# Attention heads taken in pairs with products by turns, and GpSimd's work given to VectorE

## The chip, the cores and the metric

One core of a Trainium2 chip runs the whole program. The metric is the device time of one execution in microseconds (us), the median over runs. PE is TensorE's matmul, PEld its weight load, DVE VectorE, ACT ScalarE, POOL GpSimd, SP SyncE, which issues the DMAs.

## The reference, cut to what matters

Two blocks follow each other on one sequence of 256 tokens of width 1024, all in float32.

The first block has two layers over the 256 latent tokens and, in layer 0, 256 context tokens too. Each layer is a modulated norm, an attention, a gated residual, a modulated norm, a SwiGLU feed-forward and a gated residual. Layer 0's attention has 8 latent heads (query and key of 96 rows, 64 + 32, value of 64) and 8 neighbourhood heads (64 rows, with an added bias and a mask on the latent keys); latent queries see 512 keys, context queries the 256 context keys. Layer 1's has 16 window heads of 64 rows that share 2 key heads, with a mask, a sink that enters maximum and sum, and 512 keys.

```python
p = jax.nn.softmax(sc.astype(jnp.float32) * scale, axis=-1)
return jnp.einsum('bqhk,bkc->bqhc', p, c_kv)
```

The second block has two layers of a mixer and an expert feed-forward. The mixer has five branches: pooling, a gated convolution of 31 taps, difference attention (4 heads with two score maps of 32 rows each, out = (softmax1 - lam * softmax2) V), a short convolution and memory attention (4 heads of 64 rows against 256 memory tokens); the branches are normed and projected together. The expert feed-forward scores 128 x 128 keys, picks 16 and sums the experts' outputs.

## The kernel before, in words

Activations lie with features on the 128 partitions and tokens along the free dimension. A weight arrives as a tile of 128 x 1024 (`raw`, three buffers), ACT casts it to a rounded `hi` (L85), and DVE or POOL subtracts to get `lo` (L91); which of the two is set by a pattern such as `lo_pat = "gv"`, g for POOL and v for DVE by turns. Each product is then three matmuls: hi x hi, hi x lo, lo x hi (`mm3`, L149 to L151). Activations are split in the same way (`split`, ACT at L330 and the subtraction at L334).

The program is written once in Python; a list scheduler in the compiler places each engine's instructions by priority, about program order, and by its own estimate of times. Each engine runs its list in order, and semaphores guard the buffers of each named tile. A DMA of SP's queue that waits for a buffer holds back those behind it. `issue_after(x)` puts an instruction behind x on x's engine.

An attention step (`attend`) takes one head: two query tiles of 128 tokens, with their scores S in PSUM banks of tag A (four in all). DVE takes the row maximum (L474), scales it (L476 to L479), ACT exponentiates with a running sum (L482), DVE inverts the sum (L487) and multiplies (L489), PE transposes the 128 x 128 pieces through banks of tag C (two, L495), ACT copies them to `pts` (L498), and PE multiplies them with the values into one half (64 partitions) of a bank of tag B (L500). A plain float32 product shows as two PE records. In layer 0 (`att0`) a loop runs over 8 blocks of two heads, and within it over latent and context queries; neighbourhood heads add their bias by a product with 8 times the identity (L822), after POOL has added the mask to it (L806). In layer 1 (`att1`) a loop runs over 8 blocks of two heads that lie on rows 0 to 63 and 64 to 127. Memory heads (`memattn`, scores at L1259) use `attend` too; the difference heads have their own loop (`diff`, scores at L1221), one call for each head, placed among the mixer's steps by the list `SEQ` (d0 to d3; m0 and m1 are memory heads).

The modulation's columns are made beside all this: `mod_cols` loads 128 x 1024 (`mraw` with two buffers in the first attention, later `raw`) and DVE multiplies it twice with a row, summing the product (L457). 24 of them are spread over the first attention and the projections before it.

## Time and profile before

| what | us |
|---|---|
| median of three runs | 3173.33 |
| lowest and highest | 3170.05, 3173.34 |
| the profiled execution | 3177.91 |
| its span | 3176.1 |
| PE busy | 3037.9 (96%) |
| DVE busy | 2169.0 (68%) |
| ACT busy | 1296.0 (41%) |
| POOL busy | 403.4 (13%) |

The span runs from the first instruction to the last. Busy time is the time in which an engine has at least one instruction under way; matmuls overlap, so a full PE may still be a slow one. The granted clock is the share of full speed that TensorE was given: 1.00 is 2.4 GHz, 0.50 is 1.2 GHz, and a figure between is a mean over both. POOL's work is almost all in the first block, which ends at about 1120 us.

### The profile page before, as it was taken

The page shows a single profiled execution, that of the slowest core. Times are in us where ns is not written, and L with a number is a line of the kernel's source. Part 1 is how long each engine was busy: PE and PEld are TensorE (multiplying, and loading weights), DVE is VectorE, ACT ScalarE, POOL GpSimd, SP SyncE. Part 2 cuts the span into 40 slices and gives each one's busy share as a digit, 9 for nine tenths or more (in the row PEclk, how much of TensorE's full clock was granted, in tenths as well). Part 3 has the DMA queues.
Part 4 walks back from the last instruction along what each step waited for, and adds up shares of the span by engine and source line. Part 5 has one row for each costly group of instructions (what it writes and reads, how often), then busy time and mean ns, then how long its engine had stood idle before and what let it go on. Part 6 is the DMA issues. An engine that isn't in the chain of part 4 may idle for free.

```text
span 3176.1 us, 50064 instructions
## 1 busy us (share of the span) xinstructions
PE 3037.9 (96%) x19574; PEld 2604.6 (82%) x19574; DVE 2169.0 (68%) x4434; ACT 1296.0 (41%) x2194; POOL 403.4 (13%) x214
## 2 busy tenths in 40 slices
PE   8999999998999999899999998999989999999899
PEld 4766877787589987799999986878789999998787
DVE  5777795437564467699884478556669988447854
ACT  4464322224444422344444444443334444443343
POOL 2432344443014400000000000000000000000000
PEclk9999999999799999999999999999989999999999
DMA  7303265543025552355455544554135545554454
GB/s 251 131 21 124 89 199 195 175 146 116 10 78 195 175 176 86 102 178 180 161 170 188 186 153 163 189 179 165 60 111 176 184 162 169 188 188 146 147 189 148
DMA packets 136222, 480.43 MB, mean 151 GB/s; under 512 B 15345, under 2 KB 18161, under 8 KB 135601
## 3 DMA queue, kind: packets, MB, share of 16 engines
q1 hardware_dynamic: 135888, 476.97, 44.2%
q8 instruction: 154, 2.52, 0.3%
q14 instruction: 84, 0.68, 0.1%
q0 software_dynamic: 96, 0.26, 0.0%
HBM read 476.11 MB, written 1.05 MB: 150 GB/s over the span
## 4 chain that ended last, share of the span: by engine, by line
PE 73%; DVE 15%; DMA 5%; issue 4%; ACT 1%; POOL 1%; SPq 0%; DVEq 0%; ACTq 0%; POOLq 0%
PE A L149 7%; PE A L1413 7%; PE A L1412 7%; PE A L1414 7%; PE A L150 6%; PE A L151 6%; PE B L150 6%; PE B L149 6%; PE B L151 6%; PE A L112 4%; DMA raw<-modt 3%; PE B L500 3%; DVE lo L91 2%; PE A L1098 2%; DVE junk L457 2%
## 5 line engine op out<-in xcount | busy, mean ns | idle before, releaser
L85 ACT CAST hi<-raw 128x1024 fp32r<-128x1024 f32 (+1 forms) x733 | 765.2, 1045 | 1358.1 <-PE B L150 327.6
L91 DVE TENSOR_TENSOR lo<-raw,hi 128x1024 fp32r<-128x1024 f32 (+1 forms) x601 | 738.2, 1228 | 451.4 <-ACT hi L85 446.5
L149 PE MATMUL B<-xh,hi 128*128 128x256 f32 x2048 | 575.4, 281 | 0.0
L150 PE MATMUL B<-xl,hi 128*128 128x256 f32 x2048 | 573.1, 280 | 0.0
L151 PE MATMUL B<-xh,lo 128*128 128x256 f32 x2048 | 572.4, 279 | 0.0
L149 PE MATMUL A<-xh,hi 128*128 128x256 f32 (+1 forms) x1200 | 398.0, 334 | 23.3 <-DVE nt L516 11.0
L1413 PE MATMUL A<-hi,al 128*128 128x512 f32 x1024 | 409.5, 400 | 0.2 <-DVE al L334 0.2
L1414 PE MATMUL A<-lo,ah 128*128 128x512 f32 x1024 | 407.5, 398 | 0.0
L1412 PE MATMUL A<-hi,ah 128*128 128x512 f32 x1024 | 396.7, 399 | 4.6 <-ACT ah L330 4.6
L150 PE MATMUL A<-xl,hi 128*128 128x256 f32 (+1 forms) x1200 | 397.7, 332 | 3.5 <-DVE xl L350 2.7
L151 PE MATMUL A<-xh,lo 128*128 128x256 f32 (+1 forms) x1200 | 396.6, 331 | 2.2 <-POOL lo L91 2.2
L91 POOL TENSOR_TENSOR lo<-raw,hi 128x1024 fp32r<-128x1024 f32 (+1 forms) x132 | 324.2, 2458 | 520.5 <-ACT hi L85 520.4
L150 PEld LDWEIGHTS B<-xl,hi 128*128 128x128 f32 x2048 | 385.1, 188 | 3.8
L149 PEld LDWEIGHTS B<-xh,hi 128*128 128x128 f32 x2048 | 385.0, 188 | 3.4
L151 PEld LDWEIGHTS B<-xh,lo 128*128 128x128 f32 x2048 | 384.3, 188 | 0.0
L149 PEld LDWEIGHTS A<-xh,hi 128*128 128x128 f32 x1200 | 232.1, 194 | 48.7 <-issue 18.7
L150 PEld LDWEIGHTS A<-xl,hi 128*128 128x128 f32 x1200 | 232.6, 194 | 24.9 <-DVE xl L350 3.7
L151 PEld LDWEIGHTS A<-xh,lo 128*128 128x128 f32 x1200 | 232.7, 194 | 24.1 <-POOL lo L91 4.7
L1412 PEld LDWEIGHTS A<-hi,ah 128*128 128x128 f32 x1024 | 193.6, 189 | 47.3 <-ACT ah L330 5.3
L1414 PEld LDWEIGHTS A<-lo,ah 128*128 128x128 f32 x1024 | 194.4, 190 | 45.5
L1413 PEld LDWEIGHTS A<-hi,al 128*128 128x128 f32 x1024 | 194.3, 190 | 42.6 <-DVE al L334 1.0
L457 DVE SCALAR_TENSOR_TENSOR junk<-raw,cb 128x1024 bf16<-128x1024 f32 x80 | 124.4, 1555 | 104.4 <-DMA raw<-modt 103.4
(372 smaller groups left out, 4559.8 us busy)
## 6 DMA issues: line engine op xcount, KB each, us to landing
raw<-peer_u SPq DMA_DIRECT2D x256, 512.0 KB, 3.5
raw<-peer_v SPq DMA_DIRECT2D x256, 512.0 KB, 3.5
raw<-w_gu SPq DMA_DIRECT2D x88, 512.0 KB, 3.8
raw<-modt SPq DMA_DIRECT2D x56, 512.0 KB, 3.6
w<-w_in SPq DMA_DIRECT2D x36, 512.0 KB, 4.3
raw<-w_down SPq DMA_DIRECT2D x32, 512.0 KB, 3.6
raw<-peer_wq SPq DMA_DIRECT2D x32, 512.0 KB, 3.5
mraw<-modt SPq DMA_DIRECT2D x24, 512.0 KB, 3.7
```

What stands on the lines that cost most here:

```text
L85: nc.scalar.copy(hi[:, :w], raw[:, :w])
L91: self.last_lo = e.tensor_tensor(out=lo[:, :w], in0=raw[:, :w], in1=hi[:, :w].bitcast(FT), op=OP.subtract)
L112: mm(ps[:, :256], w[:, k * 128:k * 128 + 128], x[:, k], start=k == 0, stop=k == 7)
L149: mm(out, wh, xh, start=start, stop=False)
L150: mm(out, wh, xl, start=False, stop=False)
L151: return mm(out, wl, xh, start=False, stop=stop)
L457: nc.vector.scalar_tensor_tensor(j, raw, 1.0, self.cb[:, v], op0=OP.mult, op1=OP.mult, accum_out=self.M[:, l, b, v:v + 1])
L500: nc.tensor.matmul(o, V(k), pts[:, k], start=k == 0, stop=k == nk - 1)
L1098: nc.tensor.matmul(ps, w[:, s], ch[:, b], start=b == 0, stop=b == 1)
L1412: mm(acc[t][d], ah[:, s], hi[:, ws], start=n == 0, stop=False)
L1413: mm(acc[t][d], al[:, s], hi[:, ws], start=False, stop=False)
L1414: mm(acc[t][d], ah[:, s], lo[:, ws], start=False, stop=n == 127)
```

## The change

Heads are taken two at a time. `attend2` does for two heads what `attend` did for one, and keeps its maxima and sums for both in one small tile; the matmuls of the two heads' scores (`scores2`) and of their products with the values are put in a fixed order in which the heads take turns (`turns`). The latent heads' queries and keys are padded from 96 to 128 rows with zeros. The difference heads become two calls of two heads each, with one maximum, one scaling and one inversion for both, and `SEQ` has d0 and d1 alone. All patterns that sent a subtraction to POOL send it to DVE, as do the mask's sum, the rotation of layer 1's queries and keys, and one norm. `mraw` has one buffer where it had two; `e` has three in the first attention and four elsewhere where it had two.

```diff
-SEQ = (("cg hq mq mh hn dv d0 up d1 mn d2 po cv0 sa d3 r0 mv dh sb m0 r3 w0 dn w3 m1 g0 r2 r4 cv1 w2 cm g3 w4 g2 cn g4 w1 r1 g1").split(),
-       ("hq cg mq hn dv mh d0 up d1 sa po mv mn d2 d3 w0 dh sb m0 r3 r0 w3 dn m1 g3 cv0 r2 cv1 cm g0 w2 g2 w4 cn r4 g4 w1 r1 g1").split())
+SEQ = (("cg hq mq mh hn dv d0 up mn d1 po cv0 sa r0 mv dh sb m0 r3 w0 dn w3 m1 g0 r2 r4 cv1 w2 cm g3 w4 g2 cn g4 w1 r1 g1").split(),
+       ("hq cg mq hn dv mh d0 up sa po mv mn d1 w0 dh sb m0 r3 r0 w3 dn m1 g3 cv0 r2 cv1 cm g0 w2 g2 w4 cn r4 g4 w1 r1 g1").split())
...
-LP1 = "gv"
+LP1 = "v"
...
-QLE = "ggv"
-ALE = "gg"
-NVP = "g"
+QLE = "v"
+ALE = "vv"
+NVP = "v"
...
-        self.lo_pat = "gv"
+        self.lo_pat = "v"
...
-                self.split(xh[:, k, :T], xl[:, k, :T], t, le="g" if k % 2 else "v")
+                self.split(xh[:, k, :T], xl[:, k, :T], t, le="v")
...
-            raw = self.mp.tile([128, WCH], FT, name="mraw", bufs=2)
+            raw = self.mp.tile([128, WCH], FT, name="mraw", bufs=1)
...
+    def attend2(self, S, nk, scale, V, po, sinks=None, bufs=(4, 2)):
+
+
+        nc, ap, v = self.nc, self.atp, self.nc.vector
+        w = nk * 128
+        e = [ap.tile([128, 2, 512], FT, name="e", bufs=bufs[0]) for _ in range(2)]
+        for q in range(2):
+            st = self.sp.tile([128, 5, 2], FT, name="st2", bufs=4)
+            for g in range(2):
+                v.reduce_max(st[:, 0, g:g + 1], S[g][q], axis=AX.X)
+            if sinks is not None:
+                v.scalar_tensor_tensor(st[:, 0], st[:, 0], scale, sinks, op0=OP.mult, op1=OP.max)
+                v.tensor_scalar(st[:, 1], st[:, 0], -1.0, None, op0=OP.mult)
+            else:
+                v.tensor_scalar(st[:, 1], st[:, 0], -scale, None, op0=OP.mult)
+            for g in range(2):
+                nc.scalar.activation(e[g][:, q, :w], S[g][q], AF.Exp, bias=st[:, 1, g:g + 1], scale=scale,
+                                     accum_out=st[:, 2, g:g + 1])
+            if sinks is not None:
+                v.tensor_tensor(out=st[:, 4], in0=sinks, in1=st[:, 0], op=OP.subtract)
+                nc.scalar.activation(st[:, 4], st[:, 4], AF.Exp)
+                v.tensor_tensor(out=st[:, 2], in0=st[:, 2], in1=st[:, 4], op=OP.add)
+            v.reciprocal(st[:, 3], st[:, 2])
+            for g in range(2):
+                v.tensor_scalar(e[g][:, q, :w], e[g][:, q, :w], st[:, 3, g:g + 1], None, op0=OP.mult)
+        pts = [ap.tile([128, 4, 256], FT, name="pts", bufs=bufs[1]) for _ in range(2)]
+        for g in range(2):
+            for kp in range(nk // 2):
+                pt = self.bank("C")
+                for kk in range(2):
+                    for q in range(2):
+                        k = 2 * kp + kk
+                        nc.tensor.transpose(pt[:, kk * 256 + q * 128:kk * 256 + q * 128 + 128],
+                                            e[g][:, q, k * 128:k * 128 + 128], self.ident)
+                nc.scalar.copy(pts[g][:, 2 * kp:2 * kp + 2].rearrange("p a b -> p (a b)"), pt)
+        self.turns([(po[g * 64:g * 64 + 64, :256], V(g, k), pts[g][:, k], k == nk - 1, k == 0)
+                    for k in reversed(range(nk)) for g in (1, 0)])
+
+    def turns(self, todo):
+
+        prev = None
+        for out, w, x, start, stop in todo:
+            with ExitStack() as c:
+                if prev is not None:
+                    c.enter_context(self.tc.issue_after(prev.ins))
+                prev = self.nc.tensor.matmul(out, w, x, start=start, stop=stop)
+
+    def scores2(self, S, Q, K, last):
+
+        self.turns([(S[g], Q[g][a], K[g][b], a == 1, last and a + b == 0)
+                    for a, b in ((1, 0), (0, 1), (0, 0)) for g in (1, 0)])
...
-                e = V if (2 * k + v) % 3 else nc.gpsimd
+                e = V
...
-            mq = ap.tile([96, 8, 512], FT, name="mq")
-            mk = ap.tile([96, 8, 512], FT, name="mk")
+            mq = ap.tile([128, 8, 512], FT, name="mq")
+            mk = ap.tile([128, 8, 512], FT, name="mk")
+            for m in (mq, mk):
+                nc.gpsimd.memset(m[96:128], 0.0)
...
+                    heads = [2 * (blk % 4) + g for g in range(2)]
+                    if blk < 4:
+                        qk = [parts(mq[:, h], mk[:, h], 128) for h in heads]
+                        scale, vv, rows = 96.0 ** -0.5, mv, [slice(0, 128)] * 2
+                    else:
+                        scale, vv, rows = 0.125, nv, [slice(0, 64), slice(64, 128)]
                     for cs, part in ((0, "l"), (256, "c")):
                         po = self.bank("B")
+                        nkc, k0 = (2, 2) if part == "c" else (4, 0)
+                        bias = None
+                        if blk >= 4 and part == "l":
+                            bias = []
+                            for h in heads:
+                                bt = bp.tile([128, 2, 256], FT, name="bias", bufs=2)
+                                nc.sync.dma_start(bt, i["na_bias"][h])
+                                nc.vector.tensor_tensor(out=bt, in0=bt, in1=mask[:, None].to_broadcast([128, 2, 256]),
                                                         op=OP.add)
+                                bias.append(bt)
+                        S = [[], []]
+                        if part == "c":
+                            sb = [self.bank("A") for _ in range(2)]
+                        for q in range(2):
+                            if part == "l":
+                                sb = [self.bank("A") for _ in range(2)]
+                            qs, ks = slice(cs + q * 128, cs + q * 128 + 128), slice(k0 * 128, 512)
+                            o = slice(0, 512) if part == "l" else slice(q * 256, q * 256 + 256)
+                            self.scores2([x[:, o] for x in sb], [(qk[g][0][rows[g], qs], qk[g][1][rows[g], qs])
+                                                                 for g in range(2)],
+                                         [(qk[g][2][rows[g], ks], qk[g][3][rows[g], ks]) for g in range(2)],
                                          bias is None)
+                            for g in range(2):
                                 if bias is not None:
+                                    nc.tensor.matmul(sb[g][:, 0:256], id8, bias[g][:, q], start=False, stop=True)
+                                S[g].append(sb[g][:, o])
+                        self.attend2(S, nkc, scale, lambda g, k: vv[:, k0 + k, heads[g] * 64:heads[g] * 64 + 64], po,
+                                     bufs=(3, 2))
...
-                nc.gpsimd.tensor_tensor(out=t, in0=t, in1=sin, op=OP.mult)
+                nc.vector.tensor_tensor(out=t, in0=t, in1=sin, op=OP.mult)
...
+                for qc in range(2):
+                    sb = [self.bank("A") for _ in range(2)]
+                    qs = slice(qc * 128, qc * 128 + 128)
+                    rows = [slice(g * 64, g * 64 + 64) for g in range(2)]
+                    self.scores2(sb, [(qh[r, b, qs], ql[r, b, qs]) for r in rows], [(kh[r], kl[r]) for r in rows], False)
+                    c0 = (1 - qc) * 128
+                    for g in range(2):
+                        nc.tensor.matmul(sb[g][:, c0:c0 + 128], idb, maskb[:, qc], start=False, stop=True)
+                        S[g].append(sb[g])
+                self.attend2(S, 4, 0.125, lambda g, k: v[:, k, g * 64:g * 64 + 64], po,
+                             sinks=sink.rearrange("p (g b) -> p b g", g=2)[:, b])
...
+        def heads(b):
+
+            po = self.bank("B")
+            hs = [slice(64 * b + 32 * g, 64 * b + 32 * g + 32) for g in range(2)]
+            a = [p.tile([128, 2, 256], FT, name="da", bufs=2) for _ in range(2)]
             for q in range(2):
+                S = [self.bank("A") for _ in range(2)]
+                self.turns([(S[g][:, j * 256:j * 256 + 256], qkn[hs[g], j, q * 128:q * 128 + 128], qkn[hs[g], 2 + j],
+                             True, True) for j in (1, 0) for g in (1, 0)])
+                e = p.tile([128, 4, 256], FT, name="de", bufs=2)
+                st = self.sp.tile([128, 4, 4], FT, name="st4", bufs=3)
+                for g in range(2):
+                    nc.vector.scalar_tensor_tensor(e[:, 2 * g:2 * g + 2], dist[:, q, None, :].to_broadcast([128, 2, 256]),
+                                                   -slopes[2 * b + g] / scale, S[g].rearrange("p (a b) -> p a b", a=2),
+                                                   op0=OP.mult, op1=OP.add)
+                nc.vector.reduce_max(st[:, 0], e, axis=AX.X)
+                nc.vector.tensor_scalar(st[:, 1], st[:, 0], -scale, None, op0=OP.mult)
+                for j in range(4):
+                    nc.scalar.activation(e[:, j], e[:, j], AF.Exp, bias=st[:, 1, j:j + 1], scale=scale,
+                                         accum_out=st[:, 2, j:j + 1])
+                nc.vector.reciprocal(st[:, 3], st[:, 2])
+                for g in range(2):
+                    x, y = 2 * g, 2 * g + 1
+                    nc.vector.tensor_scalar(e[:, y], e[:, y], st[:, 3, y:y + 1], lam, op0=OP.mult, op1=OP.mult)
+                    nc.vector.scalar_tensor_tensor(a[g][:, q], e[:, x], st[:, 3, x:x + 1], e[:, y],
+                                                   op0=OP.mult, op1=OP.add)
+            pts = []
+            for g in range(2):
+                pt = self.bank("C")
+                for k in range(2):
+                    for q in range(2):
+                        nc.tensor.transpose(pt[:, k * 256 + q * 128:k * 256 + q * 128 + 128],
+                                            a[g][:, q, k * 128:k * 128 + 128], self.ident)
+                pts.append(p.tile([128, 2, 256], FT, name="dpt", bufs=2))
+                nc.scalar.copy(pts[g].rearrange("p a b -> p (a b)"), pt)
+            self.turns([(po[g * 64:g * 64 + 64, :256], dv[:, k, (2 * b + g) * 64:(2 * b + g) * 64 + 64], pts[g][:, k],
+                         k == 1, k == 0) for k in (1, 0) for g in (1, 0)])
+            nc.scalar.copy(ot[:, b], po[:, :256])
+        return heads, [(ot[:, b], cat[:, 4 + b], self.c64, sub) for b in range(2)]
...
+        hs = [slice(g * 64, g * 64 + 64) for g in range(2)]
+        sb = [self.bank("A") for _ in range(2)]
+        self.turns([(sb[g][:, q * 256:q * 256 + 256], mqn[hs[g], b, q * 128:q * 128 + 128], self.mkT[hs[g], b], True, True)
+                    for q in (1, 0) for g in (1, 0)])
+        S = [[x[:, q * 256:q * 256 + 256] for q in range(2)] for x in sb]
+        self.attend2(S, 2, 0.125, lambda g, k: self.mv[:, k, (2 * b + g) * 64:(2 * b + g) * 64 + 64], po)
```

## Rows read from the trace of the kernel before

**Rows 1.** The page, its first part (engines) and its fourth (chain by engine).

```profile
PE 3037.9 (96%) x19574; PEld 2604.6 (82%) x19574; DVE 2169.0 (68%) x4434; ACT 1296.0 (41%) x2194; POOL 403.4 (13%) x214
PE 73%; DVE 15%; DMA 5%; issue 4%; ACT 1%; POOL 1%; SPq 0%; DVEq 0%; ACTq 0%; POOLq 0%
```

**Rows 2.** Engines by stretch: stretch, length, PE, PEld, DVE, ACT, POOL, clock, DMA.

```profile
141.00:303.00 162.00, 155.77 (x733) 100.58 (x732) 117.49 (x262) 90.08 (x227) 58.49 (x37) 0.98 0.23 76
303.00:605.00 302.00, 284.02 (x1352) 236.96 (x1350) 216.01 (x307) 74.05 (x101) 122.59 (x48) 0.98 0.49 167
705.00:795.00 90.00, 76.34 (x471) 68.06 (x469) 62.48 (x124) 37.36 (x71) 32.62 (x22) 0.94 0.32 114
795.00:907.00 112.00, 104.48 (x434) 60.98 (x434) 57.48 (x168) 52.20 (x135) 6.03 (x8) 0.83 0.02 6
2190.00:2290.00 100.00, 95.92 (x450) 75.34 (x449) 77.35 (x281) 29.44 (x87) 0.00 (x0) 0.91 0.24 84
```

**Rows 3.** Order of time, PE: start us, length us, instruction, count; four places.

```profile
1230.18 2.10 PE L1259 MATMUL A<-mkT,mqn 64*128 64x256 f32 x16
...
1178.39 1.99 PE L1221 MATMUL A<-qkn 32*128 32x256 f32 x8
...
844.50 1.94 PE L500 MATMUL B<-pts,v 128*64 128x256 f32 x8
846.37 0.50 PE L151 MATMUL A<-kh,ql 64*128 64x512 f32 x1
...
847.88 0.50 PE L149 MATMUL A<-kh,qh 64*128 64x512 f32 x1
848.22 0.39 PE L150 MATMUL A<-kl,qh 64*128 64x512 f32 x1
```

**Rows 4.** PE groups by line and shape, 141:303, then 795:907.

```profile
L500 PE MATMUL B<-pts,nv 128*64 128x256 f32 x96 | 25.2, 392 | 0.1
...
L500 PE MATMUL B<-pts,v 128*64 128x256 f32 x128 | 36.4, 422 | 0.3
L149 PE MATMUL A<-kh,qh 64*128 64x512 f32 x29 | 17.4, 600 | 6.4 <-ACT e L482 5.0 <-ACT qr L895 1.3
```

**Rows 5.** DVE groups by line and shape, 141 to 303: count, busy, mean ns.

```profile
L457 DVE SCALAR_TENSOR_TENSOR junk<-mraw,cb 128x1024 bf16<-128x1024 f32 x26 | 36.9, 1444 | 8.5 <-DMA mraw<-modt 8.5
L489 DVE TENSOR_SCALAR e<-e,st 128x256 f32<-128x256 f32 x32 | 16.8, 566 | 0.2
```

**Rows 6.** Single lines over the whole run: duration ns min/median/max, first and last start.

```profile
L457 DVE SCALAR_TENSOR_TENSOR junk<-mraw,cb x48: 1199/1218/3397, 60.1 to 316.8; 128x1024 bf16<-128x1024 f32 x48
L489 DVE TENSOR_SCALAR e<-e,st x112: 340/478/2435, 173.0 to 2271.1; 128x512 f32<-128x512 f32 x64, 128x256 f32<-128x256 f32 x48
L334 DVE TENSOR_TENSOR hl<-nt,hh x44: 424/686/2894, 371.9 to 1064.2; 128x512 fp32r<-128x512 f32 x22, 128x256 fp32r<-128x256 f32 x22
L91 DVE TENSOR_TENSOR lo<-raw,hi x601: 958/1224/3383, 54.1 to 3157.4; 128x1024 fp32r<-128x1024 f32 x150, 128x768 fp32r<-128x768 f32 x1
L91 POOL TENSOR_TENSOR lo<-raw,hi x132: 1830/2401/3255, 45.9 to 1118.5; 128x1024 fp32r<-128x1024 f32 x119, 128x768 fp32r<-128x768 f32 x13
```

**Rows 7.** POOL, 141 to 303: one of the lo groups.

```profile
L334 POOL TENSOR_TENSOR lo<-mk,hi 96x512 fp32r<-96x512 f32 x8 | 13.6, 1694 | 7.6 <-ACT hi L330 7.6
```

**Rows 8.** DVE groups, 335 to 605 (first feed-forward).

```profile
L457 DVE SCALAR_TENSOR_TENSOR junk<-raw,cb 128x1024 bf16<-128x1024 f32 x71 | 108.8, 1533 | 63.4 <-DMA raw<-modt 62.4
L334 DVE TENSOR_TENSOR hl<-nt,hh 128x512 fp32r<-128x512 f32 x19 | 23.7, 1248 | 0.6
```

**Rows 9.** PE's waits, 303 to 605: total us, times, longest.

```profile
PE A L149 <- DVE nt L516: 11.0, 7, 3.2
```

**Rows 10.** Tile mraw: DVE's idle before it; its DMA (page, part 6).

```profile
  DMA mraw<-modt: 12.9, 8
...
mraw<-modt SPq DMA_DIRECT2D x24, 512.0 KB, 3.7
```

**Rows 11.** Engines by stretch, one stretch inside the second attention.

```profile
855.00:868.00 13.00, 12.91 (x34) 6.78 (x33) 8.88 (x24) 5.25 (x15) 2.91 (x4) 0.50 0.00 0
```

More of the change, by code (lines that the diff above doesn't have):

```diff
@@ L720, in q_up @@
                             self.mm3(ps[:96], hi[:, s], lo[:, s], qh[:, k], ql[:, k], k == 0, k == 1)
-                        nc.scalar.copy(mq[:, h], ps[:96])
+                        nc.scalar.copy(mq[:96, h], ps[:96])
                 def uk():
@@ L787, in att0 @@
                         po = self.bank("B")
-                        for hh in range(2):
-                            if blk < 4:
-                                h = 2 * blk + hh
-                                ps_ = slice(0, 96)
-                                if part == "l":
-                                    qk[hh] = parts(mq[:, h], mk[:, h], 96)
-                                scale = 96.0 ** -0.5
-                                V = mv
-                            else:
-                                h = 2 * (blk - 4) + hh
-                                ps_ = slice(hh * 64, hh * 64 + 64)
-                                scale = 0.125
-                                V = nv
-                            nkc, k0 = (2, 2) if part == "c" else (4, 0)
-                            bias = None
-                            if blk >= 4 and part == "l":
-                                bias = bp.tile([128, 2, 256], FT, name="bias", bufs=2)
-                                nc.sync.dma_start(bias, i["na_bias"][h])
-                                nc.gpsimd.tensor_tensor(out=bias, in0=bias, in1=mask[:, None].to_broadcast([128, 2, 256]),
-                                                        op=OP.add)
-                            S = []
-                            for q in range(2):
-                                if part == "l":
-                                    s = self.bank("A")
-                                elif q == 0:
-                                    sb = self.bank("A")
-                                    s = sb[:, 0:256]
-                                else:
-                                    s = sb[:, 256:512]
-                                qs, ks = slice(cs + q * 128, cs + q * 128 + 128), slice(k0 * 128, 512)
-                                qh, ql, kh, kl = qk[hh]
-                                self.mm3(s[:, :nkc * 128], qh[ps_, qs], ql[ps_, qs], kh[ps_, ks], kl[ps_, ks], True,
@@ L920, in att1 @@
                 po = self.bank("B")
[L921 to L933 removed]
+                S = [[], []]
+                for qc in range(2):
[9 more added lines that the diff above has]
+                             sinks=sink.rearrange("p (g b) -> p b g", g=2)[:, b])
                 self.split(oh[:, b, :256], ol[:, b, :256], po[:, :256])
@@ L1121, in mixer @@
             }
-            for k in range(4):
+            for k in range(2):
                 steps[f"d{k}"] = lambda k=k: D(k)
@@ L1248, in diff @@
-        return head, [(ot[:, b], cat[:, 4 + b], self.c64, sub) for b in range(2)]
+        def heads(b):
+            po = self.bank("B")
+            hs = [slice(64 * b + 32 * g, 64 * b + 32 * g + 32) for g in range(2)]
+            a = [p.tile([128, 2, 256], FT, name="da", bufs=2) for _ in range(2)]
+            for q in range(2):
+                S = [self.bank("A") for _ in range(2)]
[21 more added lines that the diff above has]
+                pt = self.bank("C")
+                for k in range(2):
+                    for q in range(2):
[6 more added lines that the diff above has]
+            nc.scalar.copy(ot[:, b], po[:, :256])
@@ L1252, in memattn @@
         po = self.bank("B")
-        for hh in range(2):
-            hs = slice(hh * 64, hh * 64 + 64)
-            h = 2 * b + hh
-            S = []
-            sb = self.bank("A")
-            for q in range(2):
-                nc.tensor.matmul(sb[:, q * 256:q * 256 + 256], mqn[hs, b, q * 128:q * 128 + 128],
-                                 self.mkT[hs, b], start=True, stop=True)
-                S.append(sb[:, q * 256:q * 256 + 256])
-            self.attend(S, 2, 0.125, lambda k, h=h: self.mv[:, k, h * 64:h * 64 + 64], po[hs, :256])
+        hs = [slice(g * 64, g * 64 + 64) for g in range(2)]
[4 more added lines that the diff above has]
+        self.attend2(S, 2, 0.125, lambda g, k: self.mv[:, k, (2 * b + g) * 64:(2 * b + g) * 64 + 64], po)
         nc.scalar.copy(cat[:, 8 + b], po[:, :256])
```

55 lines of the change are left out of this document (1 added, 54 removed).

## The prediction

> **What bounds the kernel now.** I read the page first: TensorE is busy for 96% of the span and makes up 73% of the chain that ended last, VectorE 15% [rows 1]. Such a share is a mean, so the second view is the table by stretch, cut where the weights that are loaded change: the first attention (141 to 303 us), the first feed-forward with the output projection before it (303 to 605), the second attention's projections (705 to 795) and heads (795 to 907), and a mixer (2190 to 2290; the one of the other layer lies at 1178 to 1273 and looks alike) [rows 2]. In each of them PE is the fullest engine: 155.8 of 162 us, 284.0 of 302, 76.3 of 90, 104.5 of 112, 95.9 of 100. Behind it DVE stands at 117.5 of 162 in the first attention and 57.5 of 112 in the second. The third view is PE in order of time, to see what a product costs [rows 3]. The fourth is DVE's single lines beside their best durations, to see what POOL costs DVE [rows 5, 6].
>
> **Products by turns.** Rows 3 hold the same kind of product in both orders. Sixteen records of the memory heads' scores, which the scheduler happened to lay with the two heads alternating between rows 0 to 63 and 64 to 127, took 2.10 us, 0.131 each. Eight records of one difference head, all on the same 32 rows, took 1.99 us, 0.249 each. So alternating row groups cost 0.53 of serial ones. The change makes that order in all pairs whose heads lie on different rows:
>
> - Scores of 64 rows by 512 columns follow each other after 0.34 us (847.88 to 848.22) [rows 3]. The second attention has 8 pairs x 2 heads x 2 query tiles x 3 = 96 of them: 96 x 0.34 x 0.47 = 15.3 us freed. The neighbourhood heads of the first attention have 48: 7.7 us, and 48 of 256 columns, priced at half: 3.8 us. The latent heads (96 rows, padded to 128) stay serial: nothing.
> - The difference heads have 32 records in each mixer: 32 x (0.249 - 0.131) = 3.8 us. The memory heads' scores alternate already: nothing.
> - Products with the values write 64 columns of the array. Eight of them took from 844.50 to 846.37, with the step to the next shape 0.234 us each [rows 3]. By turns the two heads use different columns. There are 192 records in the first attention (the row of 96 for the neighbourhood heads and an equal one for the latent heads), 128 in the second [rows 4], 32 in each mixer. No row of this trace has two column halves side by side. The ends are nothing freed, and half: 22.5, 15.0 and 3.7 us. I take half, because the row pair is the nearest row and it gave 0.53.
>
> The Trainium skill ("TensorE: Matmul & The Clock Gate", Part 3, measured speedup) has three column tiles at 2.38 times, within about 5 ns of row tiling. No run here shows it. By that page the sum would stay as it is; with columns serial it would be that of the second rival.
>
> PE's work falls to 155.8 - 22.5 - 7.7 - 3.8 = 121.8 us in the first attention and to 104.5 - 15.0 - 15.3 = 74.2 in the second.
>
> **POOL's work goes to DVE.** A weight's lo part costs 2401 ns on POOL and 1224 on DVE; but DVE's own instructions are stretched while POOL runs: a 1218 ns product has a mean of 1444 in the first attention and a maximum of 3397, and the 256-wide multiply that can take 340 has a mean of 566 [rows 5, 6]. In the first attention DVE takes over 24 lo parts of 512 columns (POOL: 1694 ns in the group shown [rows 7]) and 8 bias sums, each priced as the 512-wide subtraction whose median is 686, and 5 weights' lo: 32 x 0.686 + 5 x 1.224 = 28.1 us. It gets back at least 26 x 0.226 + 32 x 0.226 = 13.1. DVE: 117.5 + 28.1 - 13.1 = 132.5 us. So DVE is late next there, with PE at 122 and ACT at 90. The stage can't be shorter than 132; if DVE fills 90% of it, 147. I take 148: -14 us. Ends: +5 (the joined heads wait for two heads' parts before the first score, and nothing overlaps better than now) and -30 (the floor).
>
> Second attention: POOL does little there (6.0 us), DVE gains 16 small subtractions, each below the 340 ns of the 256-wide multiply, and stays near 60; PE's 74.2 is the floor. PE full for 82% of the time, since each pair is a chain score, maximum, exponential, multiply, transpose, copy, product: 90 us, -22. Ends -38 and -8 (the step waits for both heads and only PE's largest saving counts).
>
> First feed-forward: 48 lo parts x 1.224 = 58.8 come to DVE, 71 x (1.533 - 1.224) + 19 x (1.248 - 0.686) = 32.6 go [rows 6, 8], so DVE goes from 216.0 to 242 of 302 us. PE waits 11.0 us there for the gate's product on DVE [rows 9], a wait that is there while single DVE instructions are held up for 2 us. Half of it goes: -5. Ends -11 (all) and +13 (half of DVE's 26 us more falls on PE).
>
> Projections, 705 to 795: 22 POOL instructions, 32.6 us, go over to DVE at about half; PE idles 13.7 of 90. A rotation no longer passes from DVE to POOL and back: -4, ends -10 and +3. In the other stretches with POOL the lo parts are prefetched behind full PE work: nothing; without that cover DVE's half cost would show at once.
>
> Mixers: 7.5 us of PE freed in each; DVE's 77 of 100 and the joined steps' longer chain take more than half: -3 each, -6 together. Ends -15 and +10.
>
> **One buffer for mraw.** The 24 transfers take 3.7 us each; with two buffers DVE idled 12.9 us for them [rows 10]. With one, the next transfer is issued only when both products of the last are done, and SP's queue holds everything behind it: the biases, w_naqk, w_eout, the first w_gu. Ends 0 (all prefetched) and +20 (the sixteen of the attention each hold DVE, the next bound there, for 1.25 us more than now). The weights behind it have three buffers of their own, so near the lower end: +4.
>
> The padding to 128 rows, two POOL memsets and the new order of the mixer's steps cost nothing that these rows could show; POOL has nothing else to do by then.
>
> **Sum.** -14 - 22 - 5 - 4 - 6 + 4 = -47 us. The profiled execution took 3177.9 us (span 3176.1), 4.6 above the median 3173.3 of the runs (3170.1 to 3173.3). It would become 3131, the median 3126. The ends on either side, added as squares, reach from 3100 to 3164.
>
> **The rivals.**
>
> 1. *Floors reached*, 3080: every stage comes within a few us of its next engine (-27, -33, -11, -8, -14, 0). For it: PE ends most waits now. Against: DVE would have to be full for a whole attention, where it now idles for scores and exponentials.
> 2. *Columns don't overlap, or the turns aren't kept*, 3145: PE has 144 us in the first attention (-10), 89 in the second (-10), mixers -3, the rest as above: -28.
> 3. *DVE takes the gain*, 3176: the joined heads and mraw's single buffer leave the first attention as it is, feed-forward +8, mraw +10, second attention -15: +3. For it: 132.5 us of DVE work in 162, all in order. Against: half of what is added is returned by POOL's silence.
> 4. *The clock*, slower. PE at half clock is in the trace already: 0.50 granted from 855 to 868 us with PE busy 12.91 of 13 [rows 11], and 0.83 over the second attention [rows 2]. If a share s of PE's work runs at half clock, the stages take 121.8(1+s), 74.2(1+s) and twice 88.4(1+s). At s = 0.25 that is -10, -19 and +21, with the other -5 a gain of 13; at 0.4 it is +9, -8 and +48, a loss of 44: 3217. It decides from about 0.29. Now the second attention is at some 0.2 (34% of the time at half). For it: PE will wait more often in just these stages. Against: the first attention is granted 0.98 though PE idles in it.
>
> The Trainium skill (same page, Part 1) says that the throttled state is the default and that activity releases it. The granted clocks here agree; it speaks for rival 4.
>
> **Chances.** Forecast 0.52, rival 1 0.13, rival 2 0.12, rival 3 0.13, rival 4 0.10. A measurement of this kernel tells about 0.2%, 6 us, from no change. Faster: 0.52, 0.13, 0.12 and a little of rivals 3 and 4, 0.80 in all; the same 0.08, out of rival 3; slower 0.12, rivals 3 and 4. The range holds the forecast's own (3100 to 3164), rivals 1 and 2 mostly, and stops short of the slower half of rival 3 and of rival 4: 3075 to 3175.
>
> **What would show it.** Right: value products and 64-row scores starting in pairs a few ns apart; the first attention near 148 us with DVE, not PE, the fullest engine; the second near 90; no lo on POOL; the 1218 ns products without the 3 us ones. Wrong: column pairs spaced as now; a granted clock below 0.8 over an attention; DVE idle for mraw above 30 us; PE's waits in the feed-forward above 11 us.

## The result and the profile after

The changed kernel takes 3092.95 us (median of 4, 3087.02 to 3094.81), the kernel before 3173.34: ratio 0.9746, interval 0.9729 to 0.9763, a gain of 80 us where 47 were forecast. The profiled execution has a span of 3089.5 us against 3176.1, 86.6 less.

The page after, engines and chain by engine, beside [rows 1]:

```profile
PE 2949.9 (95%) x19574; PEld 2579.6 (83%) x19574; DVE 2189.5 (71%) x4619; ACT 1295.6 (42%) x2194; POOL 17.5 (1%) x23
PE 77%; DVE 16%; ACT 3%; issue 2%; DMA 2%; SPq 0%; DVEq 0%; ACTq 0%
```

The products are as many, PE is busy 88 us less. DVE got 185 instructions more and only 20.5 us more work.

To find the gain, I cut both traces at the same events (the first exponential of an attention, the last split of its output, the first and last silu of a feed-forward) and compared the pieces:

| stretch | before us | after us | difference |
|---|---|---|---|
| up to the first exponential | 170.4 | 169.6 | -0.8 |
| first attention's heads | 130.5 | 113.9 | -16.6 |
| its output projection | 44.5 | 38.0 | -6.5 |
| first feed-forward, gate and up | 242.9 | 220.1 | -22.8 |
| first feed-forward, down | 129.3 | 123.8 | -5.5 |
| second attention, projections | 58.3 | 60.0 | +1.7 |
| second attention's heads | 104.0 | 81.3 | -22.7 |
| from there to the second feed-forward's first silu | 42.2 | 38.4 | -3.8 |
| difference and memory heads, layer 0 / 1 | 122.6 / 123.2 | 122.2 / 119.1 | -0.4 / -4.1 |
| all else | 2008.2 | 2003.1 | -5.1 |

Engines by stretch after (columns as in [rows 2]): the first attention, gate and up, the second attention's projections and heads, a mixer.

```profile
142.00:285.00 143.00, 124.59 (x744) 87.86 (x743) 115.94 (x291) 88.04 (x225) 0.00 (x0) 0.98 0.23 75
347.00:567.00 220.00, 220.00 (x973) 182.15 (x972) 165.43 (x251) 54.18 (x64) 0.00 (x0) 1.00 0.67 212
691.00:751.00 60.00, 43.63 (x272) 38.77 (x272) 49.95 (x134) 30.00 (x59) 0.00 (x0) 0.88 0.38 130
751.00:832.00 81.00, 69.25 (x409) 41.93 (x409) 50.32 (x171) 46.88 (x129) 0.00 (x0) 0.86 0.00 1
2130.00:2240.00 110.00, 94.23 (x446) 75.35 (x445) 71.67 (x241) 32.10 (x90) 0.00 (x0) 0.89 0.18 63
```

Gate and up of the kernel before, by the same view:

```profile
370.00:613.00 243.00, 227.11 (x967) 183.69 (x966) 167.39 (x210) 54.15 (x65) 105.67 (x42) 0.98 0.56 190
```

After, PE is full there, 220.00 of 220. Before, it idled 15.9 us and was busy 7 us longer for the same products, at a granted clock of 0.98. (These are single executions: in the runs below that leave this stretch as the change has it, it took 220.1 to 226.6 us, so the 22.8 is the upper end.) DVE took over 50 us of lo parts and is busy 2 us *less*. Its lines say why (line, operation, names, shapes, count | busy us, mean ns of one | idle before); first before, then after:

```profile
L457 DVE SCALAR_TENSOR_TENSOR junk<-raw,cb 128x1024 bf16<-128x1024 f32 x72 | 110.0, 1528 | 69.9 <-DMA raw<-modt 68.9
L334 DVE TENSOR_TENSOR hl<-nt,hh 128x512 fp32r<-128x512 f32 x20 | 24.4, 1221 | 0.6
L332 DVE CAST hh<-nt 128x512 fp32r<-128x512 f32 x20 | 19.6, 978 | 0.4
L516 DVE TENSOR_TENSOR nt<-nt,A 128x512 f32<-128x512 f32 x20 | 13.6, 680 | 5.8 <-ACT nt L511 5.8
```

```profile
L457 DVE SCALAR_TENSOR_TENSOR junk<-raw,cb 128x1024 bf16<-128x1024 f32 x72 | 88.0, 1223 | 45.4 <-DMA raw<-modt 44.8
L91 DVE TENSOR_TENSOR lo<-raw,hi 128x1024 fp32r<-128x1024 f32 x41 | 50.0, 1221 | 10.3 <-ACT hi L85 9.1 <-PE A L150 1.1
L334 DVE TENSOR_TENSOR hl<-nt,hh 128x512 fp32r<-128x512 f32 x20 | 13.7, 686 | 0.1
L568 DVE TENSOR_TENSOR nt<-nt,A 128x512 f32<-128x512 f32 x20 | 13.6, 682 | 0.7 <-ACT nt L563 0.7
L332 DVE CAST hh<-nt 128x512 fp32r<-128x512 f32 x20 | 8.4, 422 | 0.2
```

Products, subtractions and casts between SBUF tiles are shorter by 22.0, 10.7 and 11.2 us in all; nt, which reads A in PSUM, is the same. (These durations overlap, so their sum is not the busy time.) PE's waits in that stretch of the kernel before (engine, buffer, line <- what ended it: us, times, longest) were these; after, there are none.

```profile
PE A L149 <- DVE nt L516: 11.0, 7, 3.2
PE A L149 <- DVE M L461: 3.8, 1, 3.8
PE A L151 <- POOL lo L91: 1.1, 2, 0.9
```

Value products, after: PE in order of time in the second attention, then PE's groups in the first, for [rows 3, 4].

```profile
790.88 1.95 PE L547 MATMUL B<-pts,v 128*64 128x256 f32 x16
```

```profile
L547 PE MATMUL B<-pts,mv 128*64 128x256 f32 x96 | 12.1, 388 | 5.0 <-ACT pts L536 5.0
L547 PE MATMUL B<-pts,nv 128*64 128x256 f32 x96 | 12.1, 388 | 3.6 <-ACT pts L536 3.6
```

Sixteen records take what eight took (1.94); the single records start in pairs, the two 6 to 7 ns apart, and a pair follows a pair after 216 ns. The 96 records took 25.2 us, now 12.1.

### The profile page after: what moved, and what is told of

It reads as the page before. It is cut to its first block, busy times and chain, and to the rows that moved or that the text cites. A ratio compares the mean times of both kernels' runs of the same rounds, so it can differ in the third digit from the quotient of the medians.

```text
span 3089.5 us, 49994 instructions
## 1 busy us (share of the span) xinstructions
PE 2949.9 (95%) x19574; PEld 2579.6 (83%) x19574; DVE 2189.5 (71%) x4619; ACT 1295.6 (42%) x2194; POOL 17.5 (1%) x23
## 4 chain that ended last, share of the span: by engine, by line
PE 77%; DVE 16%; ACT 3%; issue 2%; DMA 2%; SPq 0%; DVEq 0%; ACTq 0%
PE A L149 9%; PE A L150 9%; PE A L151 9%; PE A L1458 7%; PE A L1459 7%; PE A L1460 7%; PE B L150 6%; PE B L151 6%; PE B L149 6%; DVE lo L91 3%; PE A L112 3%; PE A L1147 2%; DVE act L1443 2%; DVE o L1428 2%; PE B L547 1%
## 5 line engine op out<-in xcount | busy, mean ns | idle before, releaser
L91 DVE TENSOR_TENSOR lo<-raw,hi 128x1024 fp32r<-128x1024 f32 (+1 forms) x733 | 889.9, 1214 | 492.9 <-ACT hi L85 486.4
L149 PE MATMUL B<-xh,hi 128*128 128x256 f32 x2048 | 582.3, 284 | 0.0
L150 PE MATMUL B<-xl,hi 128*128 128x256 f32 x2048 | 579.9, 283 | 0.0
L151 PE MATMUL B<-xh,lo 128*128 128x256 f32 x2048 | 579.5, 283 | 0.0
L1460 PE MATMUL A<-lo,ah 128*128 128x512 f32 x1024 | 400.5, 391 | 0.0
L150 PEld LDWEIGHTS B<-xl,hi 128*128 128x128 f32 x2048 | 392.8, 192 | 3.1
L149 PEld LDWEIGHTS B<-xh,hi 128*128 128x128 f32 x2048 | 392.5, 192 | 3.1
L151 PEld LDWEIGHTS B<-xh,lo 128*128 128x128 f32 x2048 | 392.6, 192 | 0.0
L457 DVE SCALAR_TENSOR_TENSOR junk<-raw,cb 128x1024 bf16<-128x1024 f32 x80 | 97.8, 1223 | 68.2 <-DMA raw<-modt 67.6
L149 PE MATMUL A<-hh,hi 128*128 128x256 f32 (+1 forms) x374 | 122.3, 327 | 0.6 <-DVE X L592 0.6
```

Source lines behind the costliest of these rows:

```text
L91: self.last_lo = e.tensor_tensor(out=lo[:, :w], in0=raw[:, :w], in1=hi[:, :w].bitcast(FT), op=OP.subtract)
L149: mm(out, wh, xh, start=start, stop=False)
L150: mm(out, wh, xl, start=False, stop=False)
L151: return mm(out, wl, xh, start=False, stop=stop)
L457: nc.vector.scalar_tensor_tensor(j, raw, 1.0, self.cb[:, v], op0=OP.mult, op1=OP.mult, accum_out=self.M[:, l, b, v:v + 1])
L1460: mm(acc[t][d], ah[:, s], lo[:, ws], start=False, stop=n == 127)
```

## Experiments

The theory: two gains that don't depend on each other, one from POOL's silence (the feed-forward, by DVE), one from the turns (the attentions, by PE). The rival: the joined heads give all of it, and POOL's move is a cost that they cover. All ratios are against the kernel before.

**POOL's work alone** (before, with everything of POOL's on DVE).

```diff
-LP1 = "gv"; QLE = "ggv"; ALE = "gg"; NVP = "g"; self.lo_pat = "gv"
+LP1 = "v"; QLE = "v"; ALE = "vv"; NVP = "v"; self.lo_pat = "v"
-nc.gpsimd.tensor_tensor(...)   # bias sum, rotation
+nc.vector.tensor_tensor(...)
...                             # and the splits of two norms
```

> The kernel before with POOL's subtractions, mask sums and rotations on DVE and nothing else changed (one head at a time, mraw with two buffers, the old order of the mixers). Theory A: the 23 us that the first feed-forward gained come from DVE no longer being held while POOL works, so they come without any change of the attention: gate and up stretch 243 to about 220 us with no wait of PE, its output projection and down stretch -6 and -5, second feed-forward -4; the attentions stay PE-bound and within 5 us of before. Total 3130 to 3140. Rival B: DVE has room for POOL's work only because the attention and its modulation columns were rearranged; then the total stays above 3160 and the feed-forward above 235.

3143.75 us (3139.09 to 3147.43), 0.9909 [0.989, 0.9928]: -31.5, a little less than expected. Gate and up took 221.7 us, 21 less than before; the attentions' heads stayed at 131.5 and 103.6. The rival falls: POOL's move pays by itself.

**The weights' lo parts back on POOL** (after, the rest as it is).

```diff
-LP1 = "v"; NVP = "v"; self.lo_pat = "v"
+LP1 = "gv"; NVP = "g"; self.lo_pat = "gv"
```

> The changed kernel with only the weights' lo parts by turns on POOL again (as before); heads stay joined and by turns. Theory A: the first feed-forward goes back to about 243 us, the other feed-forward parts give back 10 to 15, the two attentions keep their -17 and -23: total 3093 + 35 = 3125 to 3135. Rival B: the feed-forward stays near 220 and the total below 3105.

3140.23 us, 0.9892 [0.9873, 0.9911]: 47 over the changed kernel, more than expected, and more than all of POOL's work cost in the kernel before (31.5). Gate and up is at 239.3 again, and PE waits 10.5 us in 7 places for nt. 13 of the 47 fall ahead of the first exponential (182.7 for 169.6), where the kernel before, with that work on POOL too, took 170.4. DVE idles 39.3 us for mraw in this run, 17.9 in the changed kernel: the single mraw seems to cost more beside POOL's work, but that was not run by itself. So the two gains of the theory are not independent.

**POOL holds DVE by itself?** After, with an extra subtraction on POOL whose output nobody reads, beside every second gate and up weight of the first feed-forward.

```diff
+if self.nd % 2:
+    nc.gpsimd.tensor_tensor(out=self.dummy, in0=hi.bitcast(FT), in1=hi.bitcast(FT), op=OP.subtract)
```

> The changed kernel, all lo parts on DVE, and POOL does a subtraction of 128x1024 whose result nobody reads beside every second gate and up weight of the first feed-forward. Theory A1 (POOL holds DVE): DVE's 1224 ns products get a mean above 1400 and a maximum above 3000 again, and the gate and up stretch grows from 220 by 10 to 23 us. Rival A2 (POOL's lo was slow and kept the raw buffer longer, or came late to PE): nobody waits for POOL now, so the stretch stays at 220 within 2 us and the total at 3093.

3107.48 us, 0.9794 [0.9775, 0.9812]: 14.5 over. Gate and up went from 220.1 to 234.0 us. POOL's group, then DVE's, of that stretch (the line numbers are 1 to 5 higher in this kernel):

```profile
L96 POOL TENSOR_TENSOR dummy<-hi 128x1024 f32<-128x1024 f32 x20 | 49.2, 2459 | 193.6 <-ACT hi L86 193.6
```

```profile
L462 DVE SCALAR_TENSOR_TENSOR junk<-raw,cb 128x1024 bf16<-128x1024 f32 x72 | 98.2, 1364 | 34.6 <-DMA raw<-modt 34.1
L339 DVE TENSOR_TENSOR hl<-nt,hh 128x512 fp32r<-128x512 f32 x20 | 23.6, 1181 | 0.1
L573 DVE TENSOR_TENSOR nt<-nt,A 128x512 f32<-128x512 f32 x20 | 13.6, 681 | 0.7 <-ACT nt L568 0.7
L337 DVE CAST hh<-nt 128x512 fp32r<-128x512 f32 x20 | 10.3, 516 | 0.2
```

DVE has the same work and waits for nothing of POOL's, yet its instructions between SBUF tiles are stretched (the lo parts too, 1301 for 1221 ns), and the one that reads PSUM is not. The 11 products that overlap a subtraction of POOL's take 2170 ns on the mean, the others 1219. PE idles 7.4 us, nearly all of it for DVE's lo parts, and is busy 6.5 us longer.

**Reading or writing?** After, with constants written by POOL to the same buffer, nothing read (a one-column copy on ACT paces them).

```diff
+    nc.scalar.copy(self.dtiny, self.dummy[:, 0:1])
+    nc.gpsimd.memset(self.dummy, 0.0)
+    nc.gpsimd.memset(self.dummy, 1.0)
```

> As the run with the unread subtraction on POOL, but POOL writes constants over 128x1024 twice, beside every second gate and up weight, and reads nothing; a one-column copy on ACT paces it. If POOL holds DVE whenever it works: the 1224 ns products and 686 ns subtractions of DVE are stretched again and the stretch grows by 5 to 14 us. If only a POOL instruction that reads two inputs from SBUF holds DVE's two-input instructions: products 1224, subtractions 686, stretch within 2 us of 220.

3089.94 us (2 runs), 0.974 [0.9715, 0.9765]: nothing lost. But the constants were not spread over the stretch. Nothing ties them to the weights, and all of them ran between 324 and 382 us; for the other 190 us of gate and up (221.8 in all) POOL was silent. So this run does not say what POOL's writing costs a whole stretch. It does show DVE's instructions while POOL writes: one of the two groups of constants with its first and last start, the engines from 354 to 382 us, DVE's products, subtractions and casts there, and the casts from 383 to 574.

```profile
L97 POOL MEMSET dummy<- x22: 951/954/962, 326.4 to 380.5; 128x1024 f32 x22
354.00:382.00 28.00, 28.00 (x125) 23.22 (x124) 25.87 (x39) 8.29 (x20) 22.97 (x24) 1.00 0.69 212
L464 DVE SCALAR_TENSOR_TENSOR junk<-raw,cb 128x1024 bf16<-128x1024 f32 x12 | 14.6, 1219 | 0.1
L341 DVE TENSOR_TENSOR hl<-nt,hh 128x512 fp32r<-128x512 f32 x3 | 2.1, 687 | 0.0
L339 DVE CAST hh<-nt 128x512 fp32r<-128x512 f32 x3 | 2.3, 783 | 0.0
L339 DVE CAST hh<-nt 128x512 fp32r<-128x512 f32 x16 | 6.8, 424 | 0.1
```

POOL is busy for 23 of these 28 us and all 12 products overlap its constants, yet neither products nor subtractions are stretched. The casts are, 783 ns for 424, though there are only three. So DVE's instructions with two SBUF inputs are held while POOL reads, not while it writes; the cast, which reads one SBUF tile, is held by writing too. POOL's subtraction reads two inputs; one that reads a single input was not run.

The Trainium skill ("SBUF — State Buffer", section "SBUF: two separate sides") says that the two engines share a pair of ports under an exclusive lock, which DVE takes for an operation in a two-port performance mode, or for one with two SBUF inputs, the latter only against an operation of GpSimd that reads SBUF. The traces agree on two inputs: 1364 beside the subtractions, 1219 beside the constants, and 681 for nt, whose second input is PSUM. Whether the cast runs in such a mode, no run here shows.

**Does POOL help in the first attention?** Prediction and theory had DVE late there. After, with the heads' lo parts, bias sum and rotation on POOL again, and layer 0's rotation too, which DVE did in both kernels.

```diff
-QLE = "v"; ALE = "vv"
+QLE = "ggv"; ALE = "gg"
-nc.vector.tensor_tensor(...)   # bias sum, rotations
+nc.gpsimd.tensor_tensor(...)
...                             # and half of one norm's splits
```

> The changed kernel with the attention's own POOL work back (lo parts of queries and keys, the mask's sum, the rotation, half of one norm), weights' lo on DVE. If DVE's work bounds the first attention (the prediction's reading: 116 of 143 us busy), 20 us less on it shorten that stretch by 5 to 10 us: 3083 to 3090. Rival: the holding of DVE by POOL costs what it saves or more, stretch and total the same or up to 8 us longer. The second attention's projections: between -3 and +3.

3114.94 us, 0.9817 [0.9799, 0.9835]: 22 over, where a gain was expected, or a loss of 8 at most. The first attention's heads took 123.1 us for 113.9; 6.6 of the 22 lie ahead of the first exponential, where layer 0's rotation stands, so that part is not the old work's alone. Two DVE groups of the changed kernel, then of this one, there:

```profile
L457 DVE SCALAR_TENSOR_TENSOR junk<-mraw,cb 128x1024 bf16<-128x1024 f32 x22 | 26.6, 1217 | 9.1 <-DMA mraw<-modt 9.0
L526 DVE TENSOR_SCALAR e<-e,st 128x512 f32<-128x512 f32 x32 | 14.3, 480 | 0.2
```

```profile
L457 DVE SCALAR_TENSOR_TENSOR junk<-mraw,cb 128x1024 bf16<-128x1024 f32 x24 | 33.0, 1388 | 19.9 <-DMA mraw<-modt 19.9
L526 DVE TENSOR_SCALAR e<-e,st 128x512 f32<-128x512 f32 x32 | 25.5, 826 | 0.2
```

POOL took 44.5 us of work and DVE was still busy 117.05 us in 151.3, as long as without POOL's help (115.94 in 143.0). What POOL took off DVE, its reading gave back in longer instructions.

**The turns** (after, each list of products one head after the other; then only the value lists).

```diff
-for k in reversed(range(nk)) for g in (1, 0)])
+for g in (1, 0) for k in reversed(range(nk))])
-for a, b in ((1, 0), (0, 1), (0, 0)) for g in (1, 0)])
+for g in (1, 0) for a, b in ((1, 0), (0, 1), (0, 0))])
...                             # and so in the difference and memory heads
```

> The changed kernel with the heads still joined, but in each list of products all of one head's stand before the other's, in the scores and in the products with the values. Theory C (the turns free PE): the 16 value products of a pair take about 3.5 us instead of 1.8, 64-row scores 0.34 us each instead of a pair in 0.23; the first attention's heads go from 113.9 to 122 to 130 us, the second's from 81.3 to 95 to 102, total 3115 to 3130. Rival D (joining is what pays: fewer changes of the array's shape, four banks of scores under way): both stay within 4 us and the total below 3100.

> Only the products with the values one head after the other; scores by turns. Theory C with PE as the bound: the price of the column pairs alone, 20 us of PE in the first attention and 14 in the second, of which a part shows: +5 to +10 and +8 to +14, total 3105 to 3117. Theory C with DVE as the bound of the first attention: +0 to +3 there, +8 to +14 in the second, 3100 to 3108. Rival D: nothing.

All serial: 3131.47 us, 0.9872 [0.9856, 0.9889], 38.5 over; heads 122.9 and 105.5. Only the values serial: 3111.07 us, 0.9807 [0.9789, 0.9825], 18 over; heads 121.2 and 89.5. So undoing the turns costs the second attention all of its gain (105.5 serial, 104.0 before), and 8 of the 24 us are the values'. That doesn't make the turns the whole cause, for the granted clock differs too. The second attention by the view of [rows 2], before, all serial, only the values serial:

```profile
800.50:904.50 104.00, 99.81 (x407) 57.45 (x408) 50.77 (x154) 48.17 (x129) 3.22 (x4) 0.84 0.00 1
767.00:872.00 105.00, 92.78 (x404) 59.34 (x405) 51.03 (x171) 46.84 (x128) 0.00 (x0) 0.75 0.00 1
767.80:857.30 89.50, 78.65 (x411) 48.92 (x412) 50.93 (x171) 46.99 (x128) 0.00 (x0) 0.85 0.00 1
```

PE's busy time less the part that the clock took, (1 - clock) x length, is an estimate of its work: 83 us before, 67 all serial, 65 with the values serial, 58 after. By it joining alone took 17 us off PE and the turns 9 more, 7 of them the values'. In serial order the 17 did not reach the time: the clock's part grew by 10 us, and PE idled 12 us where it had idled 4. The lower clock came with this order in every run (0.971 over the whole run in all four; 0.976 to 0.980 in the changed kernel's), so some 20 of the 38.5 us are the clock's (an estimate: 0.007 of 3100 us).

In the first attention, 9 us are the turns'. For the other 8 the joined heads, their third `e` and POOL's silence are left; silence alone gave nothing there (131.5). The value lists of two pairs in the serial kernel, PE in order of time:

```profile
829.30 2.86 PE L547 MATMUL B<-pts,v 128*64 128x256 f32 x16
861.87 2.86 PE L547 MATMUL B<-pts,v 128*64 128x256 f32 x16
```

2.86 us, not 2 x 1.94: by the single records, the second head's first product starts 5 ns after the first head's fifth, and the next ones run beside the first head's last. Even in serial order the columns overlap where the heads meet, which is part of what joining gives.

**Mixers** (after, difference and memory heads and their order as before).

> The changed kernel with the mixers' difference and memory heads one at a time and in the old order, as before; both attentions joined. The prediction gave the mixers' pairs 3 us each: total 3099. The profiles (122.6 to 122.2 and 123.2 to 119.1 us) say 0 to 4: 3093 to 3097. If the joined steps cost the mixers something that the clock hides: below 3090.

3103.22 us (3097.63 to 3117.99), 0.9777 [0.976, 0.9793]: 10 over, and above all runs of the changed kernel. The mixers took 123.1 and 124.4 us (+0.9, +5.3); a stretch that the edit doesn't touch was longer too (gate and up 226.2). The size is read below, over all runs.

**Buffers** (after; `e` in the first attention 3 to 2; the same with mraw 1 to 2; and `e` 4, with mraw's loads in the weights' own buffers to make room).

```diff
-bufs=(3, 2))
+bufs=(2, 2))
-name="mraw", bufs=1)
+name="mraw", bufs=2)
```

> The changed kernel with two e buffers instead of three in the first attention: the next pair's exponentials wait until the last pair's transposes are done. If the third buffer carries the overlap of pairs: that stretch +5 to +12 us, total 3098 to 3105. If DVE's work bounds it: within 2 us, 3091 to 3096.

> Two e buffers as in the run before it (3099.7 us), and mraw with its two buffers again; the difference of these two is mraw's buffer alone. The prediction priced the single buffer at +4 (0 to +20): then this is 3092 to 3098. If DVE's waits for mraw (17.9 us after, 12.9 before) are all at work: 3095. If the single buffer costs nothing on the chain: 3098 to 3102.

> A fourth e buffer in the first attention, so that two whole pairs fit; its space comes from mraw, whose transfers now use the weights' raw buffers. From two to three e buffers that stretch went from 125.3 to 113.9 us. If pairs still wait for e: 105 to 110, total 3083 to 3089. If DVE (95.6 of 113.5 us busy) bounds it by now: 111 to 115, total 3089 to 3096. The other side: mods in the raw ring hold back w_naqk and w_eout and add 5 to 10 us before 170 and after 284.

With two `e`: 3099.7 us, 0.9775 [0.9759, 0.9791]; the heads take 125.3 for 113.9, PE waiting 13.2 us for exponentials (7.5 after). With mraw double as well: 3094.73, 0.9752 [0.9731, 0.9773], and DVE's idling for mraw falls from 21.7 to 3.3 us. Its heads take 122.0. So the single mraw costs 3 (heads) to 5 us (medians), and the third `e` is worth 7 (medians) to 11 (heads). The two tiles are of one size, 128 x 1024 floats; three `e` beside two mraw were not run. With four `e`: 3101.97, 0.9777 [0.9756, 0.9798]. The heads do take 110.7, but the output projection 53.3 for 38.0: its weights now queue behind mraw's loads. ACT's wait there:

```profile
ACT hi L85 <- DMA raw<-w_eout: 10.8, 5, 5.7
```

**Padding** (after, 96 rows and no memsets).

> The changed kernel with the latent heads' queries and keys at 96 rows and no memsets. The prediction gave the padding nothing: 3090 to 3096. Rival: products of 96 rows load their weights later (0.33 instead of 0.23 us for the first after a transpose), 48 lists of products, +3 to +6.

3091.76 us (3090.06 to 3104.0), 0.9758 [0.9731, 0.9784]: no difference, and the rival's 3 to 6 us did not come. This run shows something else: its mixer of layer 0, with the same code, took 116.1 us for 122.1. The changed kernel's stretch, then this one's:

```profile
1101.30:1223.40 122.10, 110.35 (x538) 89.59 (x538) 83.28 (x258) 37.76 (x101) 0.00 (x0) 0.89 0.22 77
```

```profile
1104.80:1220.90 116.10, 104.15 (x539) 85.35 (x539) 83.23 (x258) 37.82 (x102) 0.00 (x0) 0.94 0.23 82
```

The granted clock makes that difference, 0.89 for 0.94, so a mixer's gain of 3 us can't be read from two executions. But three of the profiled kernels have the old mixers (before, POOL's work alone, and the one under Mixers), and nine the new ones with all turns:

| mixer | single heads us | mean | heads by turns us | mean |
|---|---|---|---|---|
| layer 0 | 120.0 to 123.1 | 121.9 | 116.0 to 122.2 | 119.0 |
| layer 1 | 119.1 to 124.4 | 122.2 | 117.9 to 119.3 | 118.6 |

That is 2.9 and 3.6 us less. Taking off half of the time in which PE was busy at half clock (an estimate, from the traces' records of PE and clock) leaves 117.5 to 117.7 against 109.5 to 110.8 us in layer 0 and 110.6 to 111.4 against 108.5 to 109.2 in layer 1: by this estimate the new mixers are shorter in every run.

## Why the prediction was right, and where its size was off

The sign and most stages came as forecast. The measured 3093 us lies below the forecast's own ends (3100 to 3164), though, and the range holds it only because it was widened for rival 1. Of the 33 us more than forecast, 24 are the feed-forward's.

- **First attention**: -14 forecast, -16.6 measured in the heads, -19 by the prediction's own cut (143 us for 148). PE's work was sized well (121.8 us; 124.6 measured). DVE was not: 132.5 forecast, 115.9 measured. What was priced was the return on two lines, 13.1 us; with four of the 26 products now outside the stretch, some 25 us came back (117.5 + 28.1 - 4.9 - 115.9). PE, not DVE, stayed the fullest engine. So that the time came out near 148, which was DVE's work over 0.9, is luck. PE's largest waits there are for the copies and exponentials of the chain:

```profile
PE B L547 <- ACT pts L536: 8.6, 12, 1.1
PE A L547 <- ACT e L518: 7.5, 7, 4.3
```

- **Second attention**: -22 forecast, -22.7 measured. Value products fell by half as chosen (36.4 to 18.9 us), and by the prediction's own cut PE is busy for 72.7 of 89.2 us, 82% as taken, where 74.2 of 90 were forecast. What freed PE was put down to the turns; by the estimate above, joining the heads did two thirds of it.
- **First feed-forward**: the mis-sized term. "Half of it goes: -5", for the 11.0 us wait, over output projection and feed-forward's first part. Measured: -22.8 in gate and up and -6.5 in the output projection, far outside the ends given for it (-11 to +13). The step that failed is "DVE goes from 216.0 to 242": by the same cut DVE is busy 214 us after.

```profile
285.00:567.00 282.00, 278.29 (x1358) 236.57 (x1357) 213.97 (x368) 78.93 (x105) 0.00 (x0) 0.99 0.60 190
```

  The sum left out the cast (11.2 us) and the small sums of M (2.1), and it added durations that overlap in part. With no growth on DVE, all 15.9 us of PE's waits in gate and up went, not half of 11.0; the other 7 came from PE's own busy time, 5 of them by the clock (1.00 for 0.98 of 243 us). POOL's work alone gives this (221.7), and a useless POOL instruction takes up to 14 us of it back.
- **Other stretches with POOL**: "nothing" forecast; -5.5 in the down projection and -3.8 on the way to the second feed-forward. POOL's work alone gave 122.0 in the down projection too. But with the weights' lo parts back on POOL the changed kernel took some 125 there, 1 us of the 5.5, so the cause is not settled.
- **Projections**: -4 forecast, +1.7 measured. POOL's work there is gone, and PE has one new wait of 5.0 us for a lo part on DVE; the granted clock is 0.88 in both.
- **Mixers**: -3 each forecast; -0.4 and -4.1 in the two profiles, -2.9 and -3.6 on the mean of all kernels. The row and column turns work (difference scores 7.6 to 4.7 us a mixer, difference values 4.3 to 2.2), and the size was right; in the profile of the change, the clock (0.96 to 0.89 in layer 0) hides it.
- **mraw**: +4 forecast, 3 to 5 measured. DVE's 3.4 us products are gone, as forecast:

```profile
L457 DVE SCALAR_TENSOR_TENSOR junk<-mraw,cb x48: 1205/1221/1226, 63.0 to 314.6; 128x1024 bf16<-128x1024 f32 x48
```

- **Rivals.** Floors (3080) came nearest, but not as it was told: the attentions stayed 18 and 12 us above PE's work, and the surplus was the feed-forward's. Columns do overlap. DVE did not take the gain. In the change's profile the clock fell in one mixer only; the attentions were granted 0.98 and 0.86. Rival 4's cost is real all the same: it is what the serial order paid. The prediction also says that the granted clocks agree with activity releasing the throttle. [rows 11] does not show that: PE was busy for 15.95 of the 17.1 us before that stretch (836.9 to 854), at 0.99, and for 12.91 of the 13 us in it, at 0.50.

By the runs, POOL's silence alone gives 31.5 of the 80 us, and undoing the turns costs 38.5, about half of it by the clock. Some 10 are left for the joined heads with their buffers; that is a difference, not run by itself. Nor is it the only way to add up: in the changed kernel the weights' lo parts on POOL cost 47 and the heads' work 22, more than POOL cost before.

## What to carry to other kernels

Work handed to GpSimd isn't free for VectorE: before splitting elementwise work over both, look at VectorE's mean beside its minimum on every line, casts too, and price the whole return. Where two heads write different halves of a PSUM bank, issue their products by turns, and look for the next limit in the chain behind them. Read the granted clock beside every stretch that you compare, and where a test instruction really ran. A buffer that stalls one queue can still be worth it if its room goes to a tile that more waits hang on.

## What the runs showed of the hardware

- Two halves of the array's columns overlap in full: 16 records in 1.95 us for 8 in 1.94. In serial order two heads' lists still overlap where they meet (16 in 2.86 us). The Trainium skill ("TensorE: Matmul & The Clock Gate", Part 3, measured speedup) has three column tiles at 2.38 times; two here reach 2 times.
- POOL that reads two SBUF inputs stretches DVE's SBUF instructions, on the mean of a stretch, from 1.1 times (1364 for 1223) to 1.8 (1221 for 686) and 2.3 (the cast, 978 for 422). POOL that writes constants leaves DVE's products and subtractions alone (1219, 687) but not its cast (783 for 424, three of them). DVE instructions that read PSUM are not held (680 to 683).
- Some 49 us of POOL subtractions lengthened a stretch full of PE's work from 220 to 234 us (7 of the 14 are within what the stretch varies by), though PE never waits for POOL there.
- The granted clock of one stretch differs between kernels with the same code there: 0.89 and 0.94 in a mixer, 6 us of 122.
